# A two-layer attention and MLP trunk on one core: the order of wide and narrow matmuls inside an output tile

## The chip, the core and the metric

The kernel runs on one core of one Trainium2 chip, as one program in one launch. The metric is the device time of that program in microseconds (us). The kernel before takes 2236.04 us, the median of three runs (2236.01 to 2237.82).

## The reference

The input is `x` (256 tokens, width 2048) and a memory of 256 tokens. Two layers follow each other, each with an attention, an output projection and an MLP. Cut to what matters here:

```python
for layer in range(2):
    xn = rms_norm(h, norm_attn[layer])
    if layer == 0:
        proj = xn @ w_in_a[0]                 # q, k, v and the memory queries
        y_main = chunk_band_attention(q, k, v, rel_bias[0])
    else:
        kv = rms_norm(h, norm_kv) @ w_kv_shared
        proj = xn @ w_q_b[0]
        y_main = stick_breaking_attention(q, k_sb, v_sb)
    y_mem = memory_attention(qm, mem_n, w_mem_kv[layer], ...)
    h = h + concat([y_main, y_mem]) @ w_o[layer]
    h = h + square(relu(rms_norm(h, norm_mlp[layer]) @ w_mlp_in[layer])) @ w_mlp_out[layer]
```

The MLP is 2048 to 8192 and back, and it holds most of the work. All of it is computed to fp32 accuracy.

## The kernel before, in words

**Split numbers.** To keep fp32 accuracy, every weight tile and every activation is split into a high part (rounded to the type fp32r) and a low part (the rest, also fp32r). A product is then high by high, plus high by low, plus low by high. The low-by-low product is left out.

**The weight ring.** All weights come in the order in which they are used, as 768 pieces of 128x1024 (512 KB each). `prepare` loads a piece into `raw` (L145, issued on SP's queue, 5 buffers), ACT rounds it into `hi` (L150, 4 buffers) and DVE subtracts to give `lo` (L151, 4 buffers). `weights` (L156) keeps three pieces prepared ahead of the one that is handed out. So the cast of a piece into `hi` needs the buffer of the piece four places earlier, and waits until TensorE (PE) has made its last use of that buffer. The subtraction into `lo` does the same on its side.

**An output tile in the features-major form.** This is the form that the change touches. The output tile is 128 features by 256 tokens. An activation tile `act` holds, for each of 16 slices of the contraction, 512 columns: 256 columns of high part and 256 columns of low part side by side. One PSUM bank of 512 columns takes a tile. Its left half gathers high by high, and its right half gathers the two mixed products. The work comes in two half-units of 8 slices each (`half_unit`, L209), one weight piece for each half-unit:

- 8 *wide* matmuls: `hi` weights against 512 columns of `act`, into the whole bank;
- 8 *narrow* matmuls: `lo` weights against the 256 columns of high part, into the right half of the bank.

PE loads a new 128x128 weight block before each of them. After the second half-unit the bank is evacuated: ACT copies the right half to SBUF (`low_part`, L260), DVE adds the left half to it, and further work follows.

`features_major` (L234) runs the two half-units of a tile one after the other. `halves_first` (L243) runs the first half-units of `n` tiles, and then their second ones. There are 311 such tiles: 16 for each of the two output projections, 255 in the MLPs, 12 for the shared keys and 12 for the queries of layer 1. The very last tile of the kernel runs in another form (`one_bank`, L218): 48 matmuls of 256 columns each.

**The tokens-major form.** Other projections (L190) use the weights as the moving side: every matmul there has 512 columns, 12 for each weight piece.

**MLP.** For each of four chunks of 2048 hidden features, 16 `up` tiles are made and then 16 `down` tiles. The evacuation of an `up` tile squares the rectified sum (DVE L715 and L717), rounds it into the high part of `hid` (ACT L720) and subtracts for the low part (POOL L721). The first `down` tile of a chunk reads `hid` in the order of its 16 slices. Its second half-unit therefore ends with the slice of the last `up` tile.

**What sets the order.** PE runs its instructions in the order of the program (`InOrder`, L46). The order on ACT, DVE, POOL and SP is set by a scheduler, except for a few pinned instructions. Attention heads run as side work: at the end of every half-unit a call of `slot` (L172) lets each of them issue its next part.

Of the kernel before, what the change touches and what calls it, by code (L numbers as in the profile page):

```python
# [16 lines left out]
P = 128  # L17
D = 2048
T = 256
# [49 lines left out]
def trunk(  # L69
# [86 lines left out]
    def weights():  # L156
        while len(prepared) < AHEAD + 1 and state["next"] < len(stream):
            prepare()
        return prepared.popleft()
# [27 lines left out]
    def mm(o, lhs, rhs, start, stop):  # L187
        nc.tensor.matmul(o, lhs, rhs, start=start, stop=stop)
# [19 lines left out]

    def half_unit(bank, act, order, first, last):  # L209
        hi, lo = weights()  # L210
        for k8 in range(8):
            w = slice(k8 * P, (k8 + 1) * P)
            mm(bank[:], hi[:, w], act[:, order[k8], :], first and k8 == 0, False)
        for k8 in range(8):
            w = slice(k8 * P, (k8 + 1) * P)
            mm(bank[:, T:], lo[:, w], act[:, order[k8], :T], False, last and k8 == 7)

    def one_bank(act, evacuate):  # L218

# [14 lines left out]
    def features_major(act, evacuate, order=tuple(range(KT))):  # L234

        bank = ps_mm.tile([P, 512], F32, name="acc", tag="acc")
        half_unit(bank, act, order[:8], True, False)
        slot()
        half_unit(bank, act, order[8:], False, True)
        evacuate(bank)  # L240
        slot()

    def halves_first(act, n, evacuate, order=tuple(range(KT)), between=None):  # L243

        banks = []
        for _ in range(n):
            bank = ps_mm.tile([P, 512], F32, name="acc", tag="acc")
            half_unit(bank, act, order[:8], True, False)
            banks.append(bank)
            slot()  # L250
        if between is not None:
            between()
        for i in range(n):
            half_unit(banks[i], act, order[8:], False, True)
            evacuate(i, banks[i])
            slot()
# [670 lines left out]
```

## Time and profile before

| what | value |
|---|---|
| median of 3 runs | 2236.04 us |
| the profiled execution, its own time | 2238.36 us |
| span of that execution's trace | 2236.7 us |
| granted TensorE clock over the span | 0.999 of full speed |
| PE busy | 2221.2 us, 99% of the span, 12208 matmuls |
| DVE busy | 1306.4 us, 58% |
| ACT busy | 1083.1 us, 48% |
| POOL busy | 649.0 us, 29% |
| DMA engines, mean busy share | about half, 185 GB/s |

Times in the trace count from the start of the span. A row of the timeline gives the start of a group of equal instructions, how long it lasts until its last instruction ends, the engine, the line, the operation, what is written and read, and the count. Matmuls overlap: one begins before the one ahead of it has left the array. So the time that PE takes for a group is read from the start of the group to the start of the next group, not from its length. All matmuls stand under L56, the helper that records them. They are told apart by the tiles they read and by 128x512 (wide) or 128x256 (narrow).

### The profile page before, as it was taken

The numbers are of one execution on the slowest core, as the hardware profiler recorded it, in microseconds if no ns is written. First come the engines' busy times: TensorE is split into PE (matmuls) and PEld (weight loads), VectorE is DVE, ScalarE is ACT, GpSimd is POOL, SyncE is SP. The second block draws the span as 40 slices with busy tenths as digits, with TensorE's granted clock in tenths as the row PEclk, the third lists the DMA queues.
The fourth block names the chain that finished last, engine by engine and source line by source line (L and its number), as shares of the span: only waits on it lengthen the run. The fifth ranks groups of instructions, "written<-read, shape, count | busy, mean of one in ns | idle before, by whom it ended". The sixth has DMA issues, their size and how long they took to land.

```text
span 2236.7 us, 31965 instructions
## 1 busy us (share of the span) xinstructions
PE 2221.2 (99%) x12208; PEld 1928.7 (86%) x12208; DVE 1306.4 (58%) x1574; ACT 1083.1 (48%) x1572; POOL 649.0 (29%) x662
## 2 busy tenths in 40 slices
PE   8999999999999999999999999999999999999999
PEld 6888888888888888888888888888888888888888
DVE  8755556665555555555666455566555555555554
ACT  5645455544444444444555447654444444444443
POOL 6610102632222222222460111363222222222222
PEclk9999999999999999999999999999999999999999
DMA  7555555555555555555555553455555555555553
GB/s 274 189 182 163 175 176 200 195 189 182 189 191 189 183 190 187 188 188 189 188 189 187 190 188 125 140 196 186 184 189 190 188 187 188 189 188 188 189 198 131
DMA packets 117225, 414.76 MB, mean 185 GB/s; under 512 B 13136, under 2 KB 16720, under 8 KB 117072
## 3 DMA queue, kind: packets, MB, share of 16 engines
q1 hardware_dynamic: 116496, 410.63, 54.4%
q8 instruction: 95, 1.56, 0.3%
q10 hardware_dynamic: 576, 2.10, 0.3%
q14 instruction: 58, 0.48, 0.1%
HBM read 410.58 MB, written 2.10 MB: 185 GB/s over the span
## 4 chain that ended last, share of the span: by engine, by line
PE 97%; DVE 1%; POOL 1%; issue 1%; ACT 0%; DMA 0%; SPq 0%; ACTq 0%; DVEq 0%
PE acc L56 94%; PE yp L56 1%; PE tp L56 1%; PE s L56 1%; PE z L56 1%; POOL hid L721 1%; DVE mg L274 0%; DMA memc<-in_mem_t 0%; ACT hi L150 0%; DVE lo L151 0%; ACT hid L720 0%; PE stat L56 0%; ACT p L436 0%; PE inv L56 0%; SPq L145 0%
## 5 line engine op out<-in xcount | busy, mean ns | idle before, releaser
L151 DVE TENSOR_TENSOR lo<-raw,hi 128x1024 fp32r<-128x1024 f32 (+1 forms) x771 | 984.6, 1278 | 821.4 <-ACT hi L150 820.6
L150 ACT CAST hi<-raw 128x1024 fp32r<-128x1024 f32 (+1 forms) x771 | 806.0, 1046 | 1084.2 <-PE acc L56 832.3
L56 PE MATMUL acc<-hid,hi 128*128 128x512 f32 (+1 forms) x2064 | 516.8, 391 | 3.7 <-POOL hid L721 3.7
L56 PE MATMUL acc<-mlpx,hi 128*128 128x512 f32 x2048 | 513.2, 392 | 0.0
L56 PEld LDWEIGHTS acc<-hid,hi 128*128 128x128 f32 x2064 | 370.4, 189 | 72.1 <-POOL hid L721 7.1
L56 PEld LDWEIGHTS acc<-mlpx,hi 128*128 128x128 f32 x2048 | 368.5, 189 | 65.9
L721 POOL TENSOR_TENSOR hid<-upsq,hid 128x256 fp32r<-128x256 f32 x128 | 188.3, 1471 | 536.3 <-ACT hid L720 536.3
L56 PEld LDWEIGHTS acc<-hid,lo 128*128 128x128 f32 x2048 | 280.3, 190 | 19.5
L56 PEld LDWEIGHTS acc<-mlpx,lo 128*128 128x128 f32 x2048 | 279.4, 190 | 20.0
L56 PE MATMUL acc<-hid,lo 128*128 128x256 f32 x2048 | 287.9, 282 | 0.0
L56 PE MATMUL acc<-mlpx,lo 128*128 128x256 f32 x2048 | 285.6, 282 | 0.0
L734 POOL TENSOR_TENSOR dn<-dn,r_mlp 128x256 f32<-128x256 f32 x127 | 94.1, 741 | 469.8 <-DVE dn L733 469.8
L56 PE MATMUL acc<-hi,xg 128*128 128x512 f32 x640 | 210.5, 399 | 0.0
L56 PEld LDWEIGHTS acc<-hi,xg 128*128 128x128 f32 x640 | 120.2, 188 | 24.7
L56 PE MATMUL acc<-y,hi 128*128 128x512 f32 x512 | 129.3, 394 | 0.0
L56 PE MATMUL acc<-lo,xg 128*128 128x512 f32 x320 | 124.7, 390 | 0.0
L260 ACT COPY low<-acc 128x256 f32<-128x256 f32 x311 | 115.9, 373 | 5.2 <-PE acc L56 5.2
L56 PEld LDWEIGHTS acc<-y,hi 128*128 128x128 f32 x512 | 92.1, 189 | 16.6
L735 POOL TENSOR_TENSOR h<-h,dn 128x256 f32<-128x256 f32 x127 | 93.6, 737 | 10.0
L56 PE MATMUL acc<-hi,mg 128*128 128x512 f32 x256 | 84.6, 408 | 0.7 <-ACT mg L272 0.5
L350 POOL TENSOR_TENSOR sroot<-msq,neg_half 128x4 f32<-128x4 f32 x20 | 28.1, 1407 | 164.5 <-DVE msq L346 164.5
L56 PEld LDWEIGHTS acc<-y,lo 128*128 128x128 f32 x512 | 69.8, 190 | 5.0
(154 smaller groups left out, 1743.6 us busy)
## 6 DMA issues: line engine op xcount, KB each, us to landing
raw<-in_w_up SPq DMA_DIRECT2D x256, 512.0 KB, 3.3
raw<-in_w_down SPq DMA_DIRECT2D x256, 512.0 KB, 3.3
raw<-in_w_in SPq DMA_DIRECT2D x80, 512.0 KB, 3.3
raw<-in_w_o SPq DMA_DIRECT2D x64, 512.0 KB, 3.3
raw<-in_w_mem SPq DMA_DIRECT2D x29, 512.0 KB, 4.3
raw<-in_w_kv_v SPq DMA_DIRECT2D x24, 512.0 KB, 3.4
raw<-in_w_kv_k SPq DMA_DIRECT2D x24, 512.0 KB, 4.3
raw<-in_w_q SPq DMA_DIRECT2D x24, 512.0 KB, 3.3
```

The source lines that it names most:

```text
L56: return self._tc.keep_in_program_order(fn(*args, **kwargs))
L150: nc.scalar.copy(hi[:, part], raw[:, part])
L151: nc.vector.tensor_tensor(lo[:, part], raw[:, part], hi[:, part].bitcast(F32), op=ALU.subtract)
L260: nc.scalar.copy(low[:], bank[:, T:])
L350: nc.gpsimd.tensor_tensor(s[:], ms[:], neg_half[:], op=ALU.pow)
L721: nc.gpsimd.tensor_tensor(hid[:, f, T:], a[:], hid[:, f, :T].bitcast(F32), op=ALU.subtract)
L734: nc.gpsimd.tensor_tensor(t[:], t[:], inv["r2"][:], op=ALU.mult)
L735: nc.gpsimd.tensor_tensor(h(o), h(o), t[:], op=ALU.add)
```

## The change

The first half-unit of a tile still issues its wide matmuls and then its narrow ones. The second half-unit now issues the narrow ones first and then the wide ones. The flag that closes the accumulation moves from the last narrow matmul to the last wide one.

```diff
     def half_unit(bank, act, order, first, last):
         hi, lo = weights()
-        for k8 in range(8):
-            w = slice(k8 * P, (k8 + 1) * P)
-            mm(bank[:], hi[:, w], act[:, order[k8], :], first and k8 == 0, False)
-        for k8 in range(8):
-            w = slice(k8 * P, (k8 + 1) * P)
-            mm(bank[:, T:], lo[:, w], act[:, order[k8], :T], False, last and k8 == 7)
+
+        def wide_ones():
+            for k8 in range(8):
+                w = slice(k8 * P, (k8 + 1) * P)
+                mm(
+                    bank[:], hi[:, w], act[:, order[k8], :],
+                    first and k8 == 0, last and k8 == 7,
+                )
+
+        def narrow_ones():
+            for k8 in range(8):
+                w = slice(k8 * P, (k8 + 1) * P)
+                mm(bank[:, T:], lo[:, w], act[:, order[k8], :T], False, False)
+
+
+        if first:
+            wide_ones()
+            narrow_ones()
+        else:
+            narrow_ones()
+            wide_ones()
```

No instruction is added or taken away. Below is PE's order where the last `up` tile of the second MLP chunk of layer 0 ends and the first `down` tile begins. `mlpx` is the MLP's input, `hid_1` its hidden activations, `hi` and `lo` are numbered buffers of the weight ring. What an instruction waits for stands in brackets: Activation is ACT, Pool is POOL. Before:

```order
L56 MATMUL acc<-mlpx_3125,hi_6474 128x512 [waits Activation_49]
L56 MATMUL acc<-mlpx_3125,hi_6474 128x512 x7
L56 MATMUL acc<-mlpx_3125,lo_6475 128x256 [waits DVE_49]
L56 MATMUL acc<-mlpx_3125,lo_6475 128x256 x7
L56 MATMUL acc<-hid_1_5729,hi_6496 128x512 [waits Activation_49,Pool_49]
L56 MATMUL acc<-hid_1_5729,hi_6496 128x512 [waits Pool_49] x7
L56 MATMUL acc<-hid_1_5729,lo_6497 128x256 [waits DVE_49]
L56 MATMUL acc<-hid_1_5729,lo_6497 128x256 x7
L56 MATMUL acc<-hid_1_5729,hi_6527 128x512 [waits Activation_49,Pool_49]
L56 MATMUL acc<-hid_1_5729,hi_6527 128x512 [waits Pool_49] x7
L56 MATMUL acc<-hid_1_5729,lo_6528 128x256 [waits DVE_49]
L56 MATMUL acc<-hid_1_5729,lo_6528 128x256 x7
```

And with the change:

```order
L56 MATMUL acc<-mlpx_3125,lo_6475 128x256 [waits DVE_49]
L56 MATMUL acc<-mlpx_3125,lo_6475 128x256 x7
L56 MATMUL acc<-mlpx_3125,hi_6474 128x512 [waits Activation_49]
L56 MATMUL acc<-mlpx_3125,hi_6474 128x512 x7
L56 MATMUL acc<-hid_1_5729,hi_6496 128x512 [waits Activation_49,Pool_49]
L56 MATMUL acc<-hid_1_5729,hi_6496 128x512 [waits Pool_49] x7
L56 MATMUL acc<-hid_1_5729,lo_6497 128x256 [waits DVE_49]
L56 MATMUL acc<-hid_1_5729,lo_6497 128x256 x7
L56 MATMUL acc<-hid_1_5729,lo_6528 128x256 [waits DVE_49]
L56 MATMUL acc<-hid_1_5729,lo_6528 128x256 x5
L56 MATMUL acc<-hid_1_5729,lo_6528 128x256 [waits Activation_49] x2
L56 MATMUL acc<-hid_1_5729,hi_6527 128x512 [waits Pool_49] x8
```

Wide ones now follow wide ones across the border of two tiles, and narrow ones follow narrow ones in the middle of a tile. Counted over PE's whole order, a narrow matmul is followed by a wide one 589 times before and 313 times now. A wide one is followed by a narrow one 622 times before and 319 times now. The last narrow ones of the first `down` tile's second half-unit now wait for ACT's high part of the last slice of `hid`. The wide ones, which wait for POOL's low part, come after them.

The second place is ACT's order at the same border, from the cast that comes ahead of the last `up` tile's evacuation. The numbers of `hi` name the pieces in the order of the stream. Before:

```order
L150 CAST hi_6580<-raw_6579 128x1024 [waits DMAHW0_49,PE_49,Activation_49]
L260 COPY low<-acc 128x256 [waits PE_49,Activation_49]
L150 CAST hi_6602<-raw_6601 128x1024 [waits DMAHW1_49,PE_49,Activation_49]
L720 CAST hid_1_5729<-upsq 128x256 [waits DVE_49]
L150 CAST hi_6631<-raw_6630 128x1024 [waits DMAHW2_49,PE_49]
```

And with the change:

```order
L150 CAST hi_6549<-raw_6548 128x1024 [waits DMAHW7_49,PE_49,Activation_49]
L275 COPY low<-acc 128x256 [waits PE_49,Activation_49]
L150 CAST hi_6580<-raw_6579 128x1024 [waits DMAHW0_49,Activation_49]
L735 CAST hid_1_5729<-upsq 128x256 [waits DVE_49]
L150 CAST hi_6602<-raw_6601 128x1024 [waits DMAHW1_49,PE_49,Activation_49]
```

The copy `low` now stands ahead of the cast of piece 6580, and the cast into `hid` stands ahead of the cast of piece 6602. DVE's order moves in the same way: the add and the square of the evacuation (L715 and L717 before, L730 and L732 now) come ahead of the subtraction for piece 6580. On SP the stores of the last chunk's `h` move ahead of one weight load each; nothing else moves there. The side work of the attention heads keeps its places.

## Rows read from the trace of the kernel before

**Rows 1.** The profile page: PE's share, and the clock granted in 40 slices.

```profile
PE 2221.2 (99%) x12208; PEld 1928.7 (86%) x12208; DVE 1306.4 (58%) x1574; ACT 1083.1 (48%) x1572; POOL 649.0 (29%) x662
...
PEclk9999999999999999999999999999999999999999
```

**Rows 2.** PE's waits, one of them: us in total, times, longest us.

```profile
PE acc L56 <- POOL hid L721: 3.7, 8, 0.5
```

**Rows 3.** PE's timeline in an MLP, 61 half-units apart: start, length, engine, line.

```profile
550.04 2.00 PE L56 MATMUL acc<-hid,hi 128*128 128x512 f32 x8
...
717.64 2.00 PE L56 MATMUL acc<-mlpx,hi 128*128 128x512 f32 x8
719.48 1.12 PE L56 MATMUL acc<-mlpx,lo 128*128 128x256 f32 x8
```

**Rows 4.** PE's timeline: a long tokens-major run, then the first features-major tile.

```profile
1188.67 0.61 PE L56 MATMUL acc<-hi,kvx 128*128 128x512 f32 x2
...
1235.59 0.39 PE L56 MATMUL acc<-hi,kvx 128*128 128x512 f32 x1
1235.82 1.98 PE L56 MATMUL acc<-kvx,hi 128*128 128x512 f32 x8
1237.63 0.64 PE L56 MATMUL acc<-kvx,lo 128*128 128x256 f32 x4
```

**Rows 5.** PE's timeline in the kernel's last tile, matmuls of 256 columns alone.

```profile
2227.06 0.40 PE L56 MATMUL acc<-hid,hi 128*128 128x256 f32 x2
...
2232.46 0.40 PE L56 MATMUL acc<-hid,hi 128*128 128x256 f32 x2
```

**Rows 6.** PE's timeline in layer 0's output projection, after a head's side work.

```profile
372.80 2.09 PE L56 MATMUL acc<-y,hi 128*128 128x512 f32 x8
374.73 1.11 PE L56 MATMUL acc<-y,lo 128*128 128x256 f32 x8
375.68 2.00 PE L56 MATMUL acc<-y,hi 128*128 128x512 f32 x8
377.52 1.11 PE L56 MATMUL acc<-y,lo 128*128 128x256 f32 x8
```

**Rows 7.** PE's timeline in the first `down` tile of layer 0's second chunk.

```profile
720.43 2.00 PE L56 MATMUL acc<-hid,hi 128*128 128x512 f32 x8
...
723.23 1.77 PE L56 MATMUL acc<-hid,hi 128*128 128x512 f32 x7
725.46 0.50 PE L56 MATMUL acc<-hid,hi 128*128 128x512 f32 x1 [0.46 <-POOL hid L721]
...
726.75 1.08 PE L56 MATMUL acc<-hid,hi 128*128 128x512 f32 x4
```

**Rows 8.** ACT's timeline at the same place.

```profile
719.72 1.05 ACT L150 CAST hi<-raw 128x1024 fp32r<-128x1024 f32 x1 [1.44 <-issue]
720.69 0.37 ACT L260 COPY low<-acc 128x256 f32<-128x256 f32 x1
722.52 1.05 ACT L150 CAST hi<-raw 128x1024 fp32r<-128x1024 f32 x1 [1.46 <-PE acc L56]
723.47 0.40 ACT L720 CAST hid<-upsq 128x256 fp32r<-128x256 f32 x1
```

**Rows 9.** DVE's timeline at the same place.

```profile
720.80 1.23 DVE L151 TENSOR_TENSOR lo<-raw,hi 128x1024 fp32r<-128x1024 f32 x1 [1.57 <-ACT hi L150]
721.95 0.42 DVE L715 TENSOR_TENSOR up<-acc,low 128x256 f32<-128x256 f32 x1
722.47 0.42 DVE L717 SCALAR_TENSOR_TENSOR upsq<-up 128x256 f32<-128x256 f32 x1
```

**Rows 10.** POOL's timeline at the same place.

```profile
723.95 1.46 POOL L721 TENSOR_TENSOR hid<-upsq,hid 128x256 fp32r<-128x256 f32 x1 [4.12 <-ACT hid L720]
```

**Rows 11.** PE's timeline behind the last head of layer 1, in the output projection.

```profile
1435.86 2.09 PE L56 MATMUL acc<-y,hi 128*128 128x512 f32 x8
```

**Rows 12.** ACT's timeline at the same place.

```profile
1436.14 0.37 ACT L282 CAST y<-yp 128x256 fp32r<-128x256 f32 x1 [0.56 <-PE yp L56]
```

## The prediction

> **What bounds the kernel now.** I read the page first: PE is busy for 99% of the span, and the granted clock stands at its full level, 2.4 GHz, in every slice [rows 1]. So the time is PE's own stream. Only two things can shorten it: fewer nanoseconds from one matmul to the next, and fewer stalls. The page does not tell how far apart matmuls are, because a busy PE counts overlapping ones. I therefore went to PE's timeline and divided distances between starts.
>
> In an MLP, two wide groups 60 half-units apart start at 550.04 and 717.64 [rows 3]. That is 2.793 us for a half-unit: 1.84 us for its eight wide matmuls (717.64 to 719.48), and so 0.95 us for its eight narrow ones. Now compare with uniform runs. In a long tokens-major run, 207 wide matmuls (69 groups of three) take 46.92 us, 226.7 ns each [rows 4], so eight take 1.813 us. In the kernel's last tile, 45 matmuls of 256 columns take 5.40 us, 120.0 ns each [rows 5], so eight take 0.960 us. Together that is 2.773 us. **Each half-unit of the MLP takes 0.020 us more than its matmuls take in uniform runs.** The wide ones lose 0.0275 us, and the narrow ones win 0.0075 us back.
>
> Does this belong to the changes of width, or to each half-unit with its waits? One place answers: the first features-major tile behind a long wide run. Its eight wide matmuls take 1.81 us (1235.82 to 1237.63) [rows 4], although it opens a new tile and a new weight piece. Behind narrow ones the same eight take 1.84 us. So the loss is paid at a step from narrow to wide, and a wide one behind a wide one of another tile is free of it.
>
> Then PE's waits: eight times it waits for POOL's `hid` at L721 [rows 2], once in each MLP chunk. The timeline of one of them shows the price. From 723.23 to 726.75 the half-unit takes 3.52 us instead of 2.79 us [rows 7], so 0.73 us is lost, more than the 0.46 us that is put down as idle, since PE also needs a moment to get going. The reason is in the order of the other engines. The evacuation of the last `up` tile waits on DVE behind a subtraction (720.80 to 721.95) [rows 9], then its cast into `hid` waits on ACT behind another cast (722.52 to 723.47) [rows 8], and POOL's subtraction ends at 725.41 [rows 10]. PE wanted it some 0.6 us earlier.
>
> **The change part by part.** It adds and removes no instruction.
>
> *Steps between widths.* Steps from narrow to wide fall from 589 to 313: 276 fewer, by 27.5 ns, is 7.6 us won. Steps from wide to narrow fall from 622 to 319: 303 fewer, by 7.5 ns each that the narrow ones had won, is 2.3 us lost. The net is **5.3 us won**. Does the loss of the remaining steps grow, now that 16 narrow ones come in a row? What I can see is that it doesn't depend on what came ahead of the narrow ones: behind a head's side work the wide ones take 1.93 us (372.80 to 374.73), yet eight narrow ones later the next wide ones take 1.84 us as everywhere (375.68 to 377.52) [rows 6]. Eight narrow ones are enough to bring PE to one and the same state, so I take 27.5 ns. The bounds are 0 and 55 ns, twice that for a run of twice the length; at 55 ns the 313 remaining steps would cost 8.6 us more and the net would be 3.3 us lost.
>
> The Trainium skill, "TensorE: Matmul & The Clock Gate", section "Back-to-back issue gap", gives the warm distance of isolated matmuls as columns over 2.4 GHz plus 2.5 ns: 216 ns and 109 ns by its formula, whatever stands beside them. By that rule the order of the widths would be worth nothing and the sum would be the stalls alone. The rows disagree on both counts: 227 and 120 ns, and a group of eight that takes 1.81 or 1.84 us depending on its neighbour.
>
> *The stalls at `hid`.* A tile now ends with a wide matmul, so ACT gets the end of the tile and the release of the `hi` buffer at the same moment, and the new order puts `low` first. With the durations of before: `low` from 720.69 to 721.06 as now [rows 8], add and square on DVE (0.42 us each, no subtraction ahead) to about 722.0, the cast of piece 6580 from 721.0 to 722.05, the cast into `hid` to about 722.5, POOL 1.46 us [rows 10] to about 724.1. PE's side moves too. The second half-unit begins at 723.23 [rows 7]. Its last two narrow ones need the high part at about 723.9, 1.4 us after it is there. Its last wide one needs POOL's part at 723.23 + 0.96 + 1.61 = 725.8 us, 1.7 us after it is there. So all of it goes: 8 times 0.73 is **5.8 us won**. The bounds are that nothing goes (0) and all (5.8).
>
> *The weight ring.* In a second half-unit `lo` is wanted 1.84 us earlier, and the `hi` buffer is released 0.95 us later. The cast of 6580 now ends at about 722.05 and, behind add and square, its `lo` at about 723.4, against 722.03 before [rows 9]. That piece serves the half-unit that starts three further on, at 720.43 + 3 x 2.79 = 728.8. Before, its narrow ones came at 730.65, 8.6 us after `lo`. Now they come at 728.8, some 5.4 us after it. The loads on SP follow `lo` and shift by the same 1.4 us; the stores that now stand ahead of a load wait for POOL's work on the tile, which ends before `lo` does. Cost: nothing, as long as that margin holds.
>
> *Side work.* 14 groups of a head's matmuls now stand ahead of narrow ones instead of wide ones. Behind them wide ones took 1.93 us instead of 1.84 us [rows 6]; PE's start behind side work is paid in either case, the part that looks like the step from narrow to wide (some 30 ns) is not. That is 0.4 us won, with bounds of 0.4 us either way. At the last head, `y` is needed by the last narrow one, about 0.9 us after 1435.86 [rows 11], while ACT's cast ends at 1436.51 [rows 12]: just in time. It happens twice, and 0.5 us lost each is the bound; I take 0.
>
> **The sum.** 5.3 + 5.8 + 0.4 = 11.5 us. The profiled execution (span 2236.7 us, own time 2238.36 us) becomes 2225.2 us of span; it ran 2.3 us above the median of the runs. From the median, 2236.04 us, the forecast is **2224.5 us**, 0.5% faster. A measurement of this kernel can tell about 0.2%, 4.5 us, from no change.
>
> **The rivals.**
> - *The loss at changes of width stays.* It belongs to each half-unit, or a run of 16 narrow ones leaves a longer recovery behind it. For it: no run of 16 narrow ones followed by wide ones exists in the trace. Against it: the 1.81 us behind a wide run, and the 1.84 us that comes out after eight narrow ones from two different starts. Then the stalls alone count: 2236.0 - 5.8, about 2230.2 us. This is also where the page's rule leads. At its bound of 55 ns, 2236.0 + 3.3 - 5.8 - 0.4 gives 2233.1 us.
> - *The stall at `hid` stays or moves* from POOL's low part to ACT's high part, now needed by the narrow ones. For it: that new wait is in PE's order. Against it: 1.4 us of margin from the rows. Then 2236.0 - 5.3 - 0.4 = 2230.3 us.
> - *Both stay*, and nothing moves: about 2236 us.
> - *The weights come late*, and it gets slower. Narrow ones at the head of a second half-unit wait for `lo`, on 311 tiles. It decides from 11.5 / 311 = 37 ns of wait per tile on; at 0.1 us per tile it would be 2224.5 + 31 = 2255.6 us. Against it stands the margin of 5.4 us that is left; the scheduler would have to hold a subtraction back by that much.
>
> **How the numbers follow.** The forecast has a chance of 0.78, with a range of its own of 2222.5 to 2226.5 us: side work and the last heads give about 1 us each way, and the prices come from starts read to 10 ns and the counts of steps, another 1 us. The first rival has 0.08, the second 0.07, both together 0.04, the slower one 0.03. The range 2222.0 to 2231.0 us takes in the forecast and the first two rivals' main times and leaves out the rest, under 0.2. Faster by over 0.2% (below 2231.5 us): the forecast and nearly all of the first two rivals, 0.91. Within 0.2%: 0.06. Slower by over 0.2%: 0.03.
>
> **What would show it.** Right: in an MLP, two half-units take 5.567 us instead of 5.587 us from start to start, the 16 wide ones of a run 3.65 us, of which the first eight take 1.84 us and the second eight 1.81 us, and the 16 narrow ones 1.91 us; PE no longer waits for `hid`; ACT copies `low` first and POOL ends some 1.3 us earlier at the border of a chunk. Wrong: a second half of a wide run at 1.84 us (the loss belongs to the half-unit); the first eight wide ones of a run above 1.84 us (the recovery grows); PE's waits showing `hid` of ACT or POOL eight times again; or PE waiting for `lo` in the MLP.

## The result, and the profile after

The changed kernel takes 2223.34 us, the median of six runs (2222.97 to 2225.27), against 2236.93 us before (six runs, 2235.62 to 2238.62). The ratio is 0.9941, with a 95% interval of 0.9930 to 0.9951: **0.6% faster, 13.6 us by the medians**. The forecast was 2224.5 us, in a range of 2222.0 to 2231.0 us. The line of the profile page that answers to [rows 1]:

```profile
PE 2208.4 (99%) x12208; PEld 1927.2 (87%) x12208; DVE 1393.5 (63%) x1574; ACT 1090.5 (49%) x1572; POOL 726.3 (33%) x662
```

PE is the bound as before, with the same 12208 matmuls in a span of 2221.6 us. Here are all of PE's waits in the changed kernel (us in total, times, longest). No wait for `hid` is left, neither for POOL's part [rows 2] nor for ACT's:

```profile
PE acc L56 <- DVE lo L151: 7.0, 5, 2.3
PE cold L56 <- DVE zeros L107: 1.5, 1, 1.5
PE acc L56 <- ACT hi L150: 0.6, 2, 0.4
PE acc L56 <- ACT mg L287: 0.3, 1, 0.3
```

PE's timeline of the changed kernel, at the border from the last `up` tiles to the first `down` tile of layer 0's second chunk (start, length, engine, line):

```profile
708.68 3.82 PE L56 MATMUL acc<-mlpx,hi 128*128 128x512 f32 x16
712.34 2.08 PE L56 MATMUL acc<-mlpx,lo 128*128 128x256 f32 x16
714.25 2.00 PE L56 MATMUL acc<-mlpx,hi 128*128 128x512 f32 x8
716.09 1.98 PE L56 MATMUL acc<-hid,hi 128*128 128x512 f32 x8
717.90 2.08 PE L56 MATMUL acc<-hid,lo 128*128 128x256 f32 x16
719.82 3.82 PE L56 MATMUL acc<-hid,hi 128*128 128x512 f32 x16
723.47 2.08 PE L56 MATMUL acc<-hid,lo 128*128 128x256 f32 x16
```

Sixteen wide ones take 3.66 us (708.68 to 712.34), and sixteen narrow ones 1.91 us (712.34 to 714.25). The border itself shows both halves of a wide run: the eight behind narrow ones take 1.84 us (714.25 to 716.09), the next eight, of another tile, 1.81 us (716.09 to 717.90). The first `down` tile, which lost 0.73 us before [rows 7], now runs like every other: 719.82 to 723.47 is 3.65 us for its last eight wide ones and the next tile's first eight.

The other engines at the same border: ACT, then DVE, then POOL, which answer to [rows 8 to 10].

```profile
716.34 0.37 ACT L275 COPY low<-acc 128x256 f32<-128x256 f32 x1 [2.71 <-PE acc L56]
716.61 1.05 ACT L150 CAST hi<-raw 128x1024 fp32r<-128x1024 f32 x1
717.74 0.41 ACT L735 CAST hid<-upsq 128x256 fp32r<-128x256 f32 x1
```

```profile
716.75 0.42 DVE L730 TENSOR_TENSOR up<-acc,low 128x256 f32<-128x256 f32 x1 [1.71 <-ACT low L275]
717.28 0.42 DVE L732 SCALAR_TENSOR_TENSOR upsq<-up 128x256 f32<-128x256 f32 x1
```

```profile
718.22 1.30 POOL L736 TENSOR_TENSOR hid<-upsq,hid 128x256 fp32r<-128x256 f32 x1 [4.27 <-ACT hid L735]
```

DVE goes straight on to the add, and POOL ends at 719.52, 3.43 us after the `down` tile's start. Before, it ended 4.98 us after it (725.41 against 720.43). The same two figures, to 0.01 us, come out at all eight borders of this kind.

**Where the time went.** Starts on PE's timeline, read at the first matmul of each stage, give this account of the profiled executions:

| stretch | before, us | after, us | difference |
|---|---|---|---|
| start of the span to the first output projection tile | 357.25 | 354.85 | -2.40 |
| 6 stretches of 16 `up` tiles, each | 89.39 | 89.07 | -0.32 |
| the first 16 `up` tiles of each layer, each | 89.82 | 89.50 | -0.32 |
| 7 stretches of 16 `down` tiles, each about | 90.12 | 89.07 | -1.05 |
| the last 16 `down` tiles, to the end of the span | 94.13 | 93.09 | -1.04 |
| layer 1's keys and values | 133.25 | 133.01 | -0.24 |
| layer 1's queries, with the heads | 118.06 | 117.13 | -0.93 |
| the two output projections | 93.85 and 93.26 | 93.61 and 93.01 | -0.24 and -0.25 |

Behind the first stretch the span falls from 1879.40 to 1866.72 us, by 12.68 us, and all of that is in the part that the change touches. The first stretch is not (experiment 6), and the medians carry it too.

### The profile page after: what moved, and what is told of

It is laid out like the page before. It is cut to its first block, busy times and chain, and to the rows that moved or that the text cites. A ratio compares the mean times of both kernels' runs of the same rounds, so it can differ in the third digit from the quotient of the medians.

```text
span 2221.6 us, 31947 instructions
## 1 busy us (share of the span) xinstructions
PE 2208.4 (99%) x12208; PEld 1927.2 (87%) x12208; DVE 1393.5 (63%) x1574; ACT 1090.5 (49%) x1572; POOL 726.3 (33%) x662
## 4 chain that ended last, share of the span: by engine, by line
PE 99%; DVE 0%; DMA 0%; issue 0%; SPq 0%; ACT 0%
PE acc L56 95%; PE yp L56 1%; PE tp L56 1%; PE s L56 1%; PE z L56 1%; DMA memc<-in_mem_t 0%; DVE mg L289 0%; DVE lo L151 0%; ACT mg L287 0%; SPq L145 0%; ACT hi L150 0%; PE stat L56 0%; PE inv L56 0%; PE spread L56 0%; DVE dn L756 0%
## 5 line engine op out<-in xcount | busy, mean ns | idle before, releaser
L151 DVE TENSOR_TENSOR lo<-raw,hi 128x1024 fp32r<-128x1024 f32 (+1 forms) x771 | 1054.1, 1368 | 267.6 <-ACT hi L150 254.7
L56 PE MATMUL acc<-hid,hi 128*128 128x512 f32 (+1 forms) x2064 | 491.6, 389 | 0.0
L56 PE MATMUL acc<-mlpx,hi 128*128 128x512 f32 x2048 | 490.2, 391 | 0.0
L736 POOL TENSOR_TENSOR hid<-upsq,hid 128x256 fp32r<-128x256 f32 x128 | 166.0, 1297 | 544.5 <-ACT hid L735 544.5
L56 PEld LDWEIGHTS acc<-hid,lo 128*128 128x128 f32 x2048 | 263.6, 191 | 9.9
L56 PE MATMUL acc<-hid,lo 128*128 128x256 f32 x2048 | 268.1, 283 | 0.0
L56 PE MATMUL acc<-mlpx,lo 128*128 128x256 f32 x2048 | 266.6, 283 | 0.0
L750 POOL TENSOR_TENSOR h<-h,dn 128x256 f32<-128x256 f32 x127 | 202.1, 1591 | 9.9
L730 DVE TENSOR_TENSOR up<-acc,low 128x256 f32<-128x256 f32 x128 | 54.3, 424 | 211.6 <-ACT low L275 211.6
L748 DVE TENSOR_TENSOR dn<-acc,low 128x256 f32<-128x256 f32 x127 | 54.0, 425 | 190.0 <-ACT low L275 190.0
```

What stands on the lines that cost most here:

```text
L56: return self._tc.keep_in_program_order(fn(*args, **kwargs))
L151: nc.vector.tensor_tensor(lo[:, part], raw[:, part], hi[:, part].bitcast(F32), op=ALU.subtract)
L730: nc.vector.tensor_tensor(t[:], bank[:, :T], low[:], op=ALU.add)
L736: nc.gpsimd.tensor_tensor(hid[:, f, T:], a[:], hid[:, f, :T].bitcast(F32), op=ALU.subtract)
L748: nc.vector.tensor_tensor(t[:], bank[:, :T], low[:], op=ALU.add)
L750: nc.gpsimd.tensor_tensor(h(o), h(o), t[:], op=ALU.add)
```

## The experiments

All times are medians; a ratio is to the kernel before on the same chip. In PE's timeline I also read each run's length of the 16 `up` tiles of layer 0's second chunk (no stall in them in any run), and of the 16 `down` tiles that follow:

| kernel | median, us | ratio, 95% interval | `up` tiles, us | `down` tiles, us |
|---|---|---|---|---|
| before | 2236.93 | 1 | 89.39 | 90.12 |
| the change | 2223.34 | 0.9941 [0.9930, 0.9951] | 89.07 | 89.07 |
| 1, first `down` tile only | 2230.30 | 0.9970 [0.9959, 0.9982] | 89.39 | 89.37 |
| 2, all but the first `down` tile | 2224.83 | 0.9945 [0.9931, 0.9960] | 89.07 | 89.09 |
| 3, alternating | 2231.37 | 0.9976 [0.9965, 0.9986] | 89.55 | 89.55 |
| 4, groups of four | 2237.60 | 1.0004 [0.9995, 1.0014] | 89.81 | 89.81 |
| 5, pairs of tiles | 2221.62 | 0.9933 [0.9920, 0.9947] | 88.91 | 88.91 |
| 6, the change again | 2225.05 | 0.9947 [0.9934, 0.9959] | 89.07 | 89.07 |
| 7, wide ones of a tile first | 2231.14 | 0.9977 [0.9967, 0.9986] | 89.07 | 90.03 |

From the uniform runs of [rows 4, 5], 16 tiles would take 16 x 2 x 2.773 = 88.75 us. So an `up` tile loses 40 ns before, 20 ns with the change, 10 ns in experiment 5, 50 ns in experiment 3 and 66 ns in experiment 4.

**1. Only the first `down` tile of each chunk.** `half_unit` and `features_major` get a flag, and one caller sets it:

```diff
-        if first:
+        if first or not flip:
             wide_ones()
             narrow_ones()
...
-                    features_major(hid, lambda b, o=o: down(o, b))
+                    features_major(hid, lambda b, o=o: down(o, b), flip=o == 0)
```

> Only the first down tile of each MLP chunk (8 tiles of 311) gets the new order of its second half-unit; all others keep the old one. It parts the two reasons for which PE's wait for hid can go: POOL's part is needed 0.95 us later, or the evacuation of the tile ahead ends earlier. Here only the first holds, since the up tile ahead keeps its old order. Theory (either is enough): POOL ends about 5.0 us after the start of the down tile as before, the last wide matmul needs it about 5.4 us after the start, so the wait goes: 8 x 0.74 + 8 x 0.02, about 6.1 us less than before, near 2230.5 us; PE's waits show no hid. Rival (the earlier evacuation did it): the eight waits stay at 0.3 us or more each and the time is within 2 us of before.

The `up` tiles take as long as before, and the `down` tiles 0.75 us less. POOL's row and PE's rows of that border show how close it is:

```profile
720.89 1.47 POOL L736 TENSOR_TENSOR hid<-upsq,hid 128x256 fp32r<-128x256 f32 x1 [4.12 <-ACT hid L735]
```

```profile
717.37 2.00 PE L56 MATMUL acc<-hid,hi 128*128 128x512 f32 x8
719.21 2.08 PE L56 MATMUL acc<-hid,lo 128*128 128x256 f32 x16
721.13 3.14 PE L56 MATMUL acc<-hid,hi 128*128 128x512 f32 x13
```

POOL ends at 722.36, 4.99 us after the tile's start at 717.37, just as late as before. The last wide one of the second half-unit now comes only about 5.4 us after the start, and PE does not stop. The later need is enough by itself, as the theory said.

**2. All tiles but the first `down` tile.** The same flag, turned round (`flip=o != 0`).

> The complement: every tile gets the new order but the first down tile of each chunk, which keeps wide before narrow in its second half-unit. POOL's part is needed as early as before (4.4 us after the down tile's start), but the up tile ahead is evacuated as in the changed kernel (POOL ends about 3.4 us after it). Theory (either is enough): the wait for hid goes too, and 303 tiles save 0.020 us each: 6.1 + 5.9 + 0.5 for side work, 12.5 us less than before, within 1 us of the changed kernel. Rival (the later need did it): PE waits eight times for hid as before, and the time is about 6.5 us below before.

The wait for `hid` is gone here too. The `down` tiles take 89.09 us, 0.02 us more than with the change, which is the one tile that keeps its old steps. The median is 1.49 us above that of the change, more than the 1 us that was expected. From the first output projection tile on, though, the two traces take 1866.88 and 1866.72 us, and the difference is 8 tiles by 20 ns. POOL's row at that border:

```profile
718.72 1.30 POOL L736 TENSOR_TENSOR hid<-upsq,hid 128x256 fp32r<-128x256 f32 x1 [4.26 <-ACT hid L735]
```

The `down` tile begins at 716.59, and POOL ends at 720.02, 3.43 us later, in time for a last wide one at about 4.4 us. So the earlier evacuation is enough by itself as well. The change removes this stall twice over.

**3. Wide and narrow in turn.** Groups of one in each half-unit:

```diff
+        RUN = 1
+        for g in range(0, 8, RUN):
+            if first:
+                wide_ones(g)
+                narrow_ones(g)
+            else:
+                narrow_ones(g)
+                wide_ones(g)
```

> Wide and narrow matmuls alternate one by one in every half-unit (first half: wide, narrow, wide, narrow; second half: narrow, wide, ...), so a tile has about 16 steps each way instead of one. It asks what a step costs. Theory A (each pair of steps costs a fixed 20 ns net): 14 or 15 more pairs on 311 tiles, 87 to 93 us more than the changed kernel, about 2310 to 2316 us. Theory B (what is paid is the slower run of the first five wide ones, 6.6, 9.1, 1.7, 5.8 and 4.1 ns above 226.7 ns, and a wide one that is followed by a narrow one pays only its first 6.6 ns, which the next narrow one wins back): no net cost at all, 311 x 0.020 = 6.2 us less than the changed kernel, about 2217 us.

Both theories miss. A tile loses 50 ns, against 320 ns by theory A and nothing by theory B. The 16 or so pairs of steps of a tile cost about 3 ns each, so a fixed price for a step does not hold for runs this short; but it isn't free either. PE's timeline in the `up` tiles of that kernel:

```profile
700.19 0.40 PE L56 MATMUL acc<-mlpx,hi 128*128 128x512 f32 x1
700.42 0.28 PE L56 MATMUL acc<-mlpx,lo 128*128 128x256 f32 x1
700.54 0.39 PE L56 MATMUL acc<-mlpx,hi 128*128 128x512 f32 x1
700.77 0.27 PE L56 MATMUL acc<-mlpx,lo 128*128 128x256 f32 x1
700.89 0.40 PE L56 MATMUL acc<-mlpx,hi 128*128 128x512 f32 x1
```

Two pairs take 0.70 us (700.19 to 700.89), 350 ns a pair, against 346.7 ns in uniform runs: a wide one takes some 233 ns and a narrow one some 117 ns. Neither is one of PE's two steady distances. What this kernel still wins over the kernel before is the stall at `hid`, and 1.08 us in layer 1's queries (see below).

**4. Groups of four.** The same code with `RUN = 4`.

> Wide and narrow matmuls in groups of four: first half-unit wide, narrow, wide, narrow; second half-unit narrow, wide, narrow, wide. A tile has three steps each way instead of one. Theory A (20 ns net for each pair of steps): 2 x 0.020 x 311 = 12.4 us more than the changed kernel, about 2235.7 us. Theory B (the recovery of the first five wide ones, cut off after four): two recoveries of 23.3 ns and one of 27.4 ns less 3 x 7.4 ns, 52 ns for a tile against 20 ns, 9.9 us more than the changed kernel, about 2233 us. Both: no wait for hid.

2237.60 us and 66 ns of loss for a tile, against 60 ns by theory A and 52 ns by theory B. Three pairs of steps at 22 ns are close to the 20 ns of the long runs. PE's timeline:

```profile
700.79 1.12 PE L56 MATMUL acc<-mlpx,lo 128*128 128x256 f32 x8
701.75 1.09 PE L56 MATMUL acc<-mlpx,hi 128*128 128x512 f32 x4
702.68 0.63 PE L56 MATMUL acc<-mlpx,lo 128*128 128x256 f32 x4
703.15 2.02 PE L56 MATMUL acc<-mlpx,hi 128*128 128x512 f32 x8
705.01 0.63 PE L56 MATMUL acc<-mlpx,lo 128*128 128x256 f32 x4
```

Four wide ones take 0.93 us (701.75 to 702.68), against 0.907 at the steady distance. Eight wide ones behind only four narrow ones take 1.86 us (703.15 to 705.01), more than the 1.84 us behind eight or sixteen. So a short narrow run makes the recovery longer, not shorter. That four narrow ones bring PE only part of the way to the state in which eight leave it would fit this; it is not shown.

**5. Pairs of tiles, runs of 32.** In the MLPs two tiles share the order, and the weights come in that order. `weights(2)` keeps two pieces ahead there, since two are in use.

```diff
+        for i in range(2):
+            bank = ps_mm.tile([P, 512], F32, name="acc", tag="acc")
+            hi, lo = weights(2)
+            wide_ones(bank, hi, order[:8], True)
...
+        for i in range(2):
+            narrow_ones(banks[i], los_[i], order[:8])
+            slot()
...
+        for i in range(2):
+            hi, lo = weights(2)
+            narrow_ones(banks[i], lo, order[8:])
...
+        for i in range(2):
+            wide_ones(banks[i], his_[i], order[8:], False)
+            evacuate(i, banks[i])
+            slot()
```

> In the MLPs two tiles are interleaved: the wide ones of both first half-units, the narrow ones of both, the narrow ones of both second half-units, the wide ones of both. Runs are 32 long instead of 16, and PE's order has 194 steps from wide to narrow instead of 319 and 188 from narrow to wide instead of 313. The weight ring runs two pieces ahead there instead of three, since two are in use. Theory (a step from narrow to wide costs 27.5 ns and the step back wins 7.5 ns, whatever the length of the runs): 125 pairs by 0.020 us, 2.5 us less than the changed kernel, about 2221 us; a stretch of 16 mlpx or hid tiles takes 0.16 us less than in the changed kernel, and the wide eights behind narrow ones still take 1.84 us. Rival (the recovery grows with the narrow run): the first eight of a wide run take more than 1.84 us behind 32 narrow ones, and nothing or less is won. Second rival (the shorter ring is late): PE waits for lo or hi in the MLP and the time is above the changed kernel's.

```profile
691.20 7.44 PE L56 MATMUL acc<-mlpx,hi 128*128 128x512 f32 x32
698.48 4.00 PE L56 MATMUL acc<-mlpx,lo 128*128 128x256 f32 x32
702.32 7.44 PE L56 MATMUL acc<-mlpx,hi 128*128 128x512 f32 x32
```

In this timeline 32 wide ones take 7.28 us (698.48 less 691.20; 32 x 226.7 ns is 7.253, plus one recovery of 0.0275), and 32 narrow ones 3.84 us. A stretch of 16 `up` tiles is 0.16 us shorter than with the change, as the theory said to the hundredth, and so is one of 16 `down` tiles. From the first output projection tile on, the trace takes 1864.22 us against 1866.72 us, 2.5 us less. PE does not wait for weights in the MLP: its waits for `lo` and `hi` (5.7 and 0.3 us) are those of the kernel's start. This is the fastest kernel of the study: its median is 3.4 us under that of the changed kernel beside it on the chip (experiment 6). Their intervals against before overlap, so the 2.5 us rest on the stretches.

**6. The changed kernel again.** No edit.

> The changed kernel as it is, beside the pairs on the same chip: about 2223 us. Its stretch before the first output projection tile, which the change does not touch, began 2.4 us earlier in the changed kernel's profile than in that of before. If that was chance (other waits for the first weight loads), it comes out anywhere between the two here; if the change did it, it comes out near 354.9 us again.

Its first output projection tile begins at 356.58 us, 1.73 us later than in the first profile of the very same code, and from there on both take 1866.72 us. So most of the 2.40 us in the first line of the account is chance. Up to that tile, PE, ACT, DVE and POOL run the same instructions in the same order in all nine traces, the one of before included, so the rest is not work of the change either.

The granted clock goes with the difference. From the 25th to the 37th us of the span it is 1.00 on average in the profiles of the change and of experiments 1, 2 and 7, whose first output projection tile begins at 354.82 to 355.33 us. It is 0.86 in the profiles of before and of experiments 3 to 6, where that tile begins at 356.11 to 357.25 us. [rows 1] cannot show this: its slices are 56 us wide, and a 9 stands for anything from 90% on, so the prediction's full clock in every slice is a little too strong. The 20th to the 40th us of the span, in the profiles of before, of the change, and of the change again (busy us by engine, then the clock, the DMA share and GB/s):

```profile
20.00:40.00 20.00, 16.44 (x64) 12.58 (x63) 19.22 (x18) 8.76 (x12) 19.48 (x22) 0.91 0.69 258
```

```profile
20.00:40.00 20.00, 16.40 (x71) 12.90 (x71) 20.00 (x18) 8.08 (x11) 19.53 (x22) 1.00 0.70 259
```

```profile
20.00:40.00 20.00, 16.42 (x64) 12.76 (x64) 19.22 (x17) 7.91 (x11) 18.77 (x22) 0.91 0.71 268
```

PE begins 71 matmuls in that stretch where the clock is 1.00, and 64 where it falls to its lower level, 1.2 GHz, for a part of it (0.91 on average). It waits for weights in this stretch in all three. In the profiles of before and of experiment 6 the clock falls just behind a wait of 1.9 us for `lo`; the first profile of the change has the same wait and no fall. What decides it is not shown.

**7. The wide ones of a tile first, then its narrow ones.** The old kernel with another loop in `features_major`:

```diff
-        half_unit(bank, act, order[:8], True, False)
+        pieces = []
+        for half in range(2):
+            hi, lo = weights(2)
+            pieces.append(lo)
+            for k8 in range(8):
+                w = slice(k8 * P, (k8 + 1) * P)
+                mm(bank[:], hi[:, w], act[:, order[8 * half + k8], :], half == 0 and k8 == 0, False)
         slot()
-        half_unit(bank, act, order[8:], False, True)
+        for half in range(2):
...
+                mm(
+                    bank[:, T:], pieces[half][:, w], act[:, order[8 * half + k8], :T],
+                    False, half == 1 and k8 == 7,
+                )
```

> Another way to the same runs of 16: in every tile of the features-major form the wide ones of both half-units come first, then the narrow ones of both, and a tile ends with narrow ones as before. PE's order has 311 steps from wide to narrow and 302 back, as few as the changed kernel. It parts the number of steps from everything else that narrow-first brings. Theory (the steps alone): a stretch of 16 mlpx tiles takes 0.32 us less than before, as in the changed kernel. Rival (what counts is that the second half-unit begins with narrow ones or that the tile ends with wide ones): it takes the same time as before. The wait for hid is another matter: the last wide one of the first down tile now comes 3.4 us after the tile's start, 1.0 us earlier than before, so the wait should be longer than the 0.74 us of before by up to 1.0 us in each of the 8 chunks, unless the evacuation also ends earlier; the whole is then 2236.9 - 6.1 + 0 to 8, 2231 to 2239 us, or about 2225 us if the wait is gone.

The `up` tiles take 89.07 us, the same as with the change. So the saving of 0.32 us in a stretch belongs to the number of steps, and not to narrow-first or to the tile's end. The wait for `hid` grows, as its last wide one comes earlier. The waits, PE's timeline and POOL's:

```profile
PE acc L56 <- POOL hid L733: 5.6, 8, 0.7
```

```profile
717.08 3.59 PE L56 MATMUL acc<-hid,hi 128*128 128x512 f32 x15
721.38 0.50 PE L56 MATMUL acc<-hid,hi 128*128 128x512 f32 x1 [0.70 <-POOL hid L733]
721.71 2.07 PE L56 MATMUL acc<-hid,lo 128*128 128x256 f32 x16
```

```profile
720.60 0.72 POOL L733 TENSOR_TENSOR hid<-upsq,hid 128x256 fp32r<-128x256 f32 x1 [4.83 <-ACT hid L732]
```

The 16 wide ones take 4.63 us (717.08 to 721.71) instead of 3.65, so 0.98 us is lost in each chunk, against 0.73 us before. The need comes 1.0 us earlier, but POOL also ends earlier, at 721.32, 4.24 us after the tile's start instead of 4.98 us; so the loss grows by 0.25 us only. This kernel has all the savings of the steps, and that wait alone keeps it 7.8 us behind the change (1874.49 against 1866.72 us from the first output projection tile on).

## Why the prediction was right

**The loss at changes of width.** Right in kind, and a little small. The `up` stretches save 0.32 us for 16 tiles, 20 ns a tile, and the sum over all 311 tiles is about 6.1 us, as the stretches show it: 5.1 in the MLPs, 0.24 each at layer 1's keys and queries (at the queries this is 12 tiles by 20 ns), 0.5 in the two output projections. The prediction had 5.3 us from counted steps and 0.4 us for side work; no run takes the side work apart. ([rows 3] calls its two wide groups 61 half-units apart. From start to start they are 60, and the prediction divides by 60.) The recovery did not grow: behind 16 narrow ones, and behind 32, the wide ones lose the same 27.5 ns as behind 8. That was the open choice between 27.5 and 55 ns, and the step that carried it (two different starts, one state after eight narrow ones) held. Experiment 4 bears it out at its edge: behind four narrow ones the state is another one. Experiment 7 gets the same saving as the change without narrow-first, and experiment 5 half as much again (0.48 us for 16 tiles).

**The formula of the Trainium skill.** The Trainium skill, "TensorE: Matmul & The Clock Gate", section "Back-to-back issue gap", gives the distance of isolated matmuls by their columns alone. Experiments 3, 4, 5 and 7 issue the same matmuls and differ by up to 56 ns a tile, so in this stream the order counts, and a formula by columns alone misses it.

**The stall at `hid`.** Right: some 5.9 us won in 8 chunks (a `down` stretch saves 1.05 to 1.06 us, of which 0.32 us are the steps), against 5.8 us in the sum. The order read from ACT and DVE gave POOL's end at about 3.7 us after the tile's start; it came at 3.43 us, in part because POOL's subtraction took 1.30 us instead of 1.46 us. What the prediction did not say is that either reason is enough by itself (experiments 1 and 2).

**What the sum lacked.** Layer 1's queries save 0.93 us, of which 0.24 us are steps. The other 0.7 us stands in no term of the prediction. It is a wait of a head that was there once before, in PE's timeline of the kernel before, and is not in the changed kernel's:

```profile
1344.13 0.38 PE L56 MATMUL z<-sp,neg_ones 128*128 128x128 f32 x2
1345.05 0.92 PE L56 MATMUL z<-qb,kb 128*128 128x256 f32 x4 [0.54 <-ACT p L436]
```

```profile
1335.71 0.38 PE L56 MATMUL z<-sp,neg_ones 128*128 128x128 f32 x2
1335.93 0.82 PE L56 MATMUL z<-qb,kb 128*128 128x256 f32 x4
```

The two starts are 0.92 us apart before and 0.22 us after. ACT's order changed in that stage, and experiments 3, 4 and 7, whose orders changed too, save about as much there (1.08, 0.86 and 1.03 us), while experiment 1, which leaves that stage as it was, saves nothing (118.06 us). In the kernel before, ACT's `p` starts at 1343.99, straight behind a weight cast (1343.03 to 1344.08); in the changed kernel no cast stands there, and `p` is done 0.8 us ahead of the matmul. That fits, but which moved instruction does it was not tried apart.

**The weight ring** cost nothing: PE's five waits for `lo` all fall in the first 30 us of the span, and even one piece less ahead (experiment 5) was early enough in the MLPs. So the slower rival falls, and those in which a term stays fall with the stretches above.

The forecast was 11.5 us won, and the account from the trace is 12.7 us: 6.1 + 5.9 + 0.7. That the measured median lies as near as 1.2 us to the forecast is in part luck, since the start of the span alone moves the time by more; the stretches carry the two main terms.

## What to carry to other kernels

When PE is busy for 99% of the time, divide distances between starts by counts and compare a mixed stretch with uniform ones: a loss of 20 ns in 2.8 us is visible there and nowhere on the page of the profile, and runs of one width can be made longer by turning the order of every second group. Ask of a wait both when the data is needed and when it is made, and price both sides: here either of two small shifts removed it. And compare stretches rather than spans, since the start of this kernel varies by up to 2.4 us between traces that run the same instructions in it.

## What the runs showed of the hardware

**A recovery without a wait.** PE's waits list none in these stretches, and still: behind a run of eight or more narrow matmuls the first eight wide ones take 27.5 ns more than steady ones, the same behind 8, 16 and 32. The starts are 233, 236, 228, 232 and 231 ns apart in the traces, and 227 ns from the sixth on. With runs of four the price of a pair of steps stays at 22 ns, but with runs of one it falls to about 3 ns. What PE is doing in that time stays open: the weight loads between the matmuls were not tried apart.

**A stop costs more than its idle time.** At `hid` 0.46 us was put down as idle and 0.73 us was lost; in experiment 7, 0.70 us and 0.98 us.

**POOL beside DVE.** The same add on POOL takes more than twice as long in the changed kernel, by the groups of before and after (us in all, then mean ns):

```profile
L735 POOL TENSOR_TENSOR h<-h,dn 128x256 f32<-128x256 f32 x127 | 93.6, 737 | 10.0
```

```profile
L750 POOL TENSOR_TENSOR h<-h,dn 128x256 f32<-128x256 f32 x127 | 202.1, 1591 | 9.9
```

POOL's and DVE's timelines of the changed kernel show the two engines together:

```profile
723.64 1.60 POOL L750 TENSOR_TENSOR h<-h,dn 128x256 f32<-128x256 f32 x1
```

```profile
723.26 1.38 DVE L151 TENSOR_TENSOR lo<-raw,hi 128x1024 fp32r<-128x1024 f32 x1 [0.52 <-ACT hi L150]
```

DVE's subtraction begins at 723.26 and ends at 724.64, 1.38 us instead of the usual 1.23 us. POOL's add is issued under it, at 723.64, and ends at 725.24, 0.60 us after the subtraction, though it takes 0.74 us by itself. The Trainium skill, "SBUF — State Buffer", section "SBUF: two separate sides", says that a DVE instruction with two SBUF inputs and a GpSimd instruction that reads SBUF share a pair of ports under an exclusive lock, and that the later one is blocked for the whole of the other. The rows agree that the later one is held up, here by 0.86 us. By the recorded ends it is 0.14 us less than a wait for the whole subtraction would give, and no run tells whether that is the lock or how ends on POOL are recorded. It costs the kernel nothing that the trace shows: none of PE's waits comes from it.
